# Attention: score and meta products over 128 rows with zeros in the unused half, and raw weight buffers split by stage

## The chip, the cores and the metric

The kernel runs on one core of one Trainium2 chip. The metric is the device time of one execution in microseconds (us); less is better. The core has five engines that run side by side: TensorE (PE, matrix products; PEld is its loading of weights), VectorE (DVE), ScalarE (ACT), GpSimd (POOL) and SyncE (SP), which issues most DMA transfers.

## The reference, cut to what matters

One decoder block over 1,024 positions and 16 meta tokens ahead of them (1,040 keys), width 1,024: a norm, a recurrent branch and an attention branch with gates, an output projection, and an MLP. The attention has 8 heads; a head has two components of 64 dimensions, and its result is the difference of two softmaxes, applied to 128-wide values:

```
s = jnp.einsum('bqhcd,bkhcd->bhcqk', q, k) * scale        # c: the two components
p = jax.nn.softmax(jnp.where(mask, s, min), axis=-1)
p_diff = p[:, :, 0] - lam * p[:, :, 1]
return jnp.einsum('bhqk,bkhe->bqhe', p_diff, v)
```

## The kernel before, in words

Every float32 operand of a product is split into a high part and a low part of a shorter format, and a product is made of three: high by low, low by high, high by high (`mm3`). The stages follow one another: norm and transposition of the inputs, recurrent branch, its gate and projection, attention, merge, output projection, MLP.

**Weights.** `load_split` loads 1,024 numbers a partition (512 KB) into a raw buffer `w_raw` (two in turn, `WRAW`), has POOL write the high part `w_hi` and DVE (POOL in the attention stage) the low part `w_lo`, each with two buffers. `col_tile` hands out a tile and calls `load_ahead` for the next one, so loading runs one tile ahead of use. The second half of the output projection and `row_tile` of the MLP take raw buffers from the same pair.

**Scores.** The keys of a component are stored with their 64 high rows and their 64 low rows stacked in 128 rows (`k2`), and the queries' high part twice (`q2`), so that one product over 128 rows gives two of the three terms. The third one, the queries' low part by the keys' high part, runs over the 64 rows that hold them: `ql` has the low parts of both components stacked, component 0 in rows 0 to 63 and component 1 in rows 64 to 127. `scores` goes through a block of 128 queries in steps: each step is one `ql` product and one `q2` product into one of three banks (`take_s`), and a DVE instruction that adds the mask and takes the maximum. Then come the exponentials on ACT and the difference of the softmaxes on DVE (`s`).

**Values.** `turn` transposes the differences of two blocks of queries, `weigh` multiplies them by the values. The 16 meta tokens are handled apart: their high and low parts are stacked in 64 rows, and `weigh_meta` adds one product over 64 rows (`mt` by `vmt`).

**Order.** Within the attention stage PE's order is the program's order. Steps of the next head's projections (keys, values, queries, of 260 or 504 columns at a time) are placed between the steps of a head by tables written out by hand (`MAIN_FIRST`, `MAIN`, `MAIN_LAST`, `TAIL`). When a key or query projection ends, `rope` copies it, moves halves by DMA, and multiplies and adds on DVE and POOL. The other engines' order is set by a scheduler.

Of the kernel before, what the change touches and what calls it, by code (L numbers as in the profile page):

```python
# [11 lines left out]
F32 = mybir.dt.float32  # L12
F32R = mybir.dt.float32r
# [5 lines left out]
P = 128  # L19
# [14 lines left out]
# chunks of all positions and of those after the meta tokens, none across the halves  # L34
# [4 lines left out]
WRAW = 2  # L39
MZ = 464  # L40
# attention: the inputs of the next head are worked out in STEPS steps between the steps of a head;
# so many of them come after each step: of all its blocks but the last two (of the first head, of the
# last one and of the others), and of the last two. START: ahead of the first head; SPARE: kept from
# the last head for the merge
# [8 lines left out]
# steps of the second gate's projection ahead of the last sums  # L53
# [4 lines left out]
def _rope_tables():  # L58
    """cos and sin by (row of a head's two 64-wide components, position); the sine carries the
    sign of the rotation."""  # L60
    inv = (1.0 / (10000.0 ** (np.arange(0, HD, 2) / HD)).astype(np.float32)).astype(np.float32)
    ang = inv[:, None] * np.arange(T, dtype=np.float32)[None, :]
    c, s = np.cos(ang), np.sin(ang)
    return (np.concatenate([c, c, c, c]).astype(np.float32),
            np.concatenate([-s, s, -s, s]).astype(np.float32))
# [3 lines left out]
def hybrid_block(ctx: ExitStack, tc: tile.TileContext, x, meta_tokens, g_mix, w_in, conv_w, conv_b,  # L69
# [11 lines left out]
    def f32(ap):  # L81
        return ap.bitcast(F32)

    def banks_of(first, n):
        """takes the n banks of PSUM from the first on in turn; between two turns, the bank of the
        later one."""
# [19 lines left out]
    # columns of weights in the order of their use, loaded one tile ahead  # L106
# [44 lines left out]
    def mm3(o, pairs, first=True, last=True):  # L151
        """o += sum of lhsT.T @ rhs over pairs of split operands; the product of the two low parts
        lies below float32's last place."""
# [25 lines left out]
    def rstd_of(ssum, n, rows=P):  # L179
        """1 / sqrt(ssum / n + eps) of one number a partition."""  # L180
# [5 lines left out]
    # scratch in DRAM  # L186
# [6 lines left out]
    # of the heads' blocks of queries: sums of the exponentials  # L193
# [5 lines left out]
    with tc.tile_pool(name="hn", bufs=1) as hnp:  # L199
# [6 lines left out]
        with tc.tile_pool(name="pre", bufs=2) as pre:  # L206
            blocks = [(NM, 0, meta_tokens)] + [(P, NM + P * i, x[0, P * i:P * (i + 1), :]) for i in range(NB)]
            xts = []
            for i, (rows, col, src) in enumerate(blocks):
# [6 lines left out]
                if i == 4:  # L216
                    # per-channel vectors: rows of 128, turned into columns
# [40 lines left out]
            # 4 softplus(-lambda): log1p(e) = 2 atanh(e / (2 + e)) as a series in z <= 1/3  # L258
# [16 lines left out]
        def project_by(c0, chunks, take, use):  # L275
            """columns c0.. of w_in against positions, a step at a time; use(first, width, psum) takes
            each chunk."""
# [15 lines left out]
        with tc.tile_pool(name="yr", bufs=1, reuse_waits="tile") as yrp:  # L293
            yr = []
            with tc.tile_pool(name="rg", bufs=1, reuse_waits="tile") as rg, \
# [9 lines left out]
                for n in range(KT):  # L305
# [14 lines left out]
                    # gelu(x) = x sigmoid(2 sqrt(2/pi) (x + 0.044715 x^3))  # L320
# [19 lines left out]
                    # t = tanh(-log_a / 2): a = (1 - t) / (1 + t), sqrt(1 - a^2) = 2 sqrt(t) / (1 + t)  # L340
# [41 lines left out]
        with tc.tile_pool(name="atc", bufs=1, reuse_waits="tile") as atc, \  # L382
# [5 lines left out]
            # zeros, then a block of 128 with the keys after the row's own position masked  # L388
# [4 lines left out]
            # the differential weight  # L393
# [7 lines left out]
            # minus lambda, in column 0  # L401
# [6 lines left out]

            def rope(h, c0, chunks, done, E=G):
                """columns c0.. of w_in against positions, rotated by position."""  # L410
# [24 lines left out]
            def head_inputs(h):  # L435
                """keys, values and queries of a head, a step at a time."""
                # keys of a component: the 64 rows' high parts and low parts, stacked
                yield from rope(h, 3 * D + P * h, ALL, lambda t1: set_keys(h, t1))
                # values by position: high parts and low parts
# [12 lines left out]
                for step, _ in enumerate(rope(h, 2 * D + P * h, REAL, lambda t1: rot.update({h: t1}), V)):  # L452
# [5 lines left out]
                    for i, j in enumerate(js):  # L458
                        if j < NB:
                            transpose(o[:, i, :], vt[:, NM + P * j:NM + P * (j + 1)])  # L460
                        else:
                            transpose(o[:4 * NM, i, :], f32(vm).rearrange("p a b c -> p (a b c)"))
                            vt_meta[h] = at.tile([4 * NM, P], F32R, name="vmt", bufs=2)
                            A.copy(out=vt_meta[h], in_=o[:4 * NM, i, :])
# [5 lines left out]
            def queries(h):  # L470
                """queries of a component: the high parts twice; the low parts of both, stacked."""
                t1 = rot[h]
                q2 = [at.tile([P, S], F32R, name=f"q2{c}") for c in range(2)]
                ql = at.tile([P, S], F32R, name="ql")
                ques[h] = q2, ql
                for c, (own, oth) in enumerate(halfs):
                    A.copy(out=q2[c][own], in_=t1[own])
                    V.tensor_copy(out=q2[c][oth], in_=t1[own])
                    V.tensor_tensor(out=ql[own], in0=t1[own], in1=f32(q2[c][own]), op=ALU.subtract)

            def scores(h, b, st):
                """a block of queries against the keys, and the difference of its softmaxes."""
# [6 lines left out]
                for c in range(2):  # L489
                    s = at.tile([P, T], F32, name=f"s{c}", bufs=3 - c)  # L490
                    sc.append(s)
                    for i in range(np_):
# [3 lines left out]
                        q2, ql = ques[h]  # L496
                        own = halfs[c][0]
                        matmul(o[:, :wa], lhsT=ql[own, P * b:P * (b + 1)], rhs=keys[h][c][own, k0:k0 + wa],
                               start=True, stop=False)
                        matmul(o[:, :wa], lhsT=q2[c][:, P * b:P * (b + 1)], rhs=keys[h][c][:, k0:k0 + wa],  # L500
# [12 lines left out]
                # e0 - lambda (sum0 / sum1) e1: the difference times sum0  # L513
# [8 lines left out]
                # of the meta tokens: high parts twice, low parts twice  # L522
# [6 lines left out]
            def turn(p, g, st):  # L529
                """two blocks of keys of the differences of two blocks of queries, transposed; the  # L530
# [331 lines left out]
```

## Time and profile before

| | us |
|---|---|
| median of 3 runs (lowest to highest) | 2036.28 (2035.9 to 2040.91) |
| span of the profiled execution, first to last instruction | 2034.7 |
| time of the median run that is not in this span | 1.6 |
| PE busy in the span | 1964.6 (97%) |
| DVE busy | 1132.7 (56%) |
| ACT busy | 584.6 (29%) |
| POOL busy | 515.8 (25%) |

A busy PE is not a PE at its peak: matmuls are pipelined, and the record of one overlaps that of the next. Busy time tells where PE has work; how fast it works is read from the starts of its instructions. Idle time of another engine costs nothing as long as PE does not wait for it.

### The profile page before, as it was taken

To read this page: it belongs to the slowest core of one execution; us is meant where nothing else is said; L and a number is where in the kernel's file an instruction comes from. 1 tells how busy PE (TensorE), PEld (TensorE's weight loads), DVE (VectorE), ACT (ScalarE), POOL (GpSimd) and SP (SyncE) were. 2 spreads that over 40 slices of the span, in tenths; PEclk is the share of its full clock that TensorE was granted. 3 is DMA by queue.
4 is the path that set the end of the run, shared out by engine and by line. 5 is a ranking of instruction groups with operands and counts; after the bars stand their busy time and mean duration, and the time that the engine had idled before them with its cause. 6 is when DMAs were issued, how large, how long until landed. Compare 5 with 4: busy or idle time off the path is not lost.

```text
span 2034.7 us, 26093 instructions
## 1 busy us (share of the span) xinstructions
PE 1964.6 (97%) x10562; PEld 1651.9 (81%) x10562; DVE 1132.7 (56%) x1909; ACT 584.6 (29%) x1190; POOL 515.8 (25%) x364
## 2 busy tenths in 40 slices
PE   7989889999999999999999999999999999999998
PEld 6988888888778778878779888878888888888886
DVE  7788882113677677667752543444444444444446
ACT  5534440002444554445433220320011110001113
POOL 3355540016242333234203332010011100111102
PEclk9999999999899999999999999999999999999999
DMA  5111112132012111111206535021111111111202
GB/s 161 38 42 32 43 32 73 63 114 77 21 48 58 40 40 50 40 37 50 60 29 217 194 121 186 1 83 42 42 52 56 48 52 42 42 42 53 63 21 83
DMA packets 138154, 131.60 MB, mean 65 GB/s; under 512 B 6081, under 2 KB 118945, under 8 KB 138033
## 3 DMA queue, kind: packets, MB, share of 16 engines
q1 hardware_dynamic: 135664, 127.83, 20.2%
q10 hardware_dynamic: 2368, 2.10, 0.4%
q8 instruction: 83, 1.36, 0.3%
q14 instruction: 39, 0.31, 0.1%
HBM read 104.61 MB, written 16.84 MB: 60 GB/s over the span
## 4 chain that ended last, share of the span: by engine, by line
PE 79%; DVE 12%; issue 4%; ACT 2%; DMA 1%; POOL 1%; SPq 0%; DVEq 0%; ACTq 0%; POOLq 0%
PE bank L142 77%; PE bank L147 2%; DVE gate L345 2%; DVE t L422 1%; DVE s L519 1%; DVE xc L313 1%; DVE cf L517 1%; DVE xcl L318 1%; DVE s L503 1%; POOL gate L344 1%; DVE yr L368 1%; DVE fin L830 0%; DVE w_lo L103 0%; ACT L343 0%; ACT s L343 0%
## 5 line engine op out<-in xcount | busy, mean ns | idle before, releaser
L142 PE MATMUL bank<-act1l,w_hi 128*128 128x260 f32 (+1 forms) x1152 | 360.5, 313 | 3.8 <-ACT sg L359 2.9
L142 PE MATMUL bank<-act1h,w_lo 128*128 128x260 f32 (+1 forms) x1152 | 358.5, 311 | 0.0
L142 PE MATMUL bank<-act1h,w_hi 128*128 128x260 f32 (+1 forms) x1152 | 358.2, 311 | 0.0
L102 POOL TENSOR_SCALAR w_hi<-w_raw 128x1024 fp32r<-128x1024 f32 x108 | 135.0, 1250 | 805.7 <-PE bank L142 722.1
L142 PE MATMUL bank<-act0l,w_hi 128*128 128x260 f32 (+2 forms) x896 | 316.2, 353 | 0.0
L142 PE MATMUL bank<-act0h,w_lo 128*128 128x260 f32 (+2 forms) x896 | 311.5, 348 | 1.2 <-DVE w_lo L103 1.2
L142 PE MATMUL bank<-act0h,w_hi 128*128 128x260 f32 (+2 forms) x896 | 311.7, 348 | 0.0
L817 DVE TENSOR_TENSOR h<-bank,h 128x512 f32<-128x512 f32 x256 | 176.4, 690 | 200.1 <-PE bank L142 200.1
L142 PEld LDWEIGHTS bank<-act1l,w_hi 128*128 128x128 f32 x1152 | 221.8, 193 | 17.0 <-ACT sg L359 3.1
L142 PEld LDWEIGHTS bank<-act1h,w_lo 128*128 128x128 f32 x1152 | 221.4, 192 | 12.6
L142 PEld LDWEIGHTS bank<-act1h,w_hi 128*128 128x128 f32 x1152 | 221.3, 192 | 11.7
L795 ACT ACTIVATE relu<-bank 128x512 f32<-128x512 f32 x64 | 38.3, 600 | 575.0 <-PE bank L142 555.2
L103 DVE TENSOR_TENSOR w_lo<-w_raw,w_hi 128x1024 fp32r<-128x1024 f32 x76 | 109.6, 1442 | 165.3 <-POOL w_hi L102 165.3
L142 PE MATMUL bank<-w_l,ff_h 128*128 128x512 f32 x512 | 200.5, 392 | 0.0
L142 PE MATMUL bank<-w_h,ff_h 128*128 128x512 f32 x512 | 200.5, 392 | 0.0
L142 PE MATMUL bank<-w_h,ff_l 128*128 128x512 f32 x512 | 199.4, 390 | 0.0
L142 PEld LDWEIGHTS bank<-act0h,w_hi 128*128 128x128 f32 x896 | 170.3, 190 | 21.6
L142 PEld LDWEIGHTS bank<-act0h,w_lo 128*128 128x128 f32 x896 | 170.6, 190 | 20.6 <-ACT sq L234 1.4
L142 PEld LDWEIGHTS bank<-act0l,w_hi 128*128 128x128 f32 x896 | 170.4, 190 | 18.8 <-DVE act0l L252 0.3
L784 POOL TENSOR_SCALAR w_h<-w_raw 128x1024 fp32r<-128x1024 f32 x32 | 34.0, 1065 | 516.3 <-PE bank L142 295.6
L503 DVE CUSTOM_DVE_ANT_0 s<-bank,mask 128x144 f32<-128x144 f32 (+6 forms) x224 | 113.0, 507 | 91.4 <-PE bank L142 90.3
L511 ACT ACTIVATE s<-s,m 128x272 f32<-128x272 f32 (+7 forms) x128 | 100.0, 784 | 63.2 <-DVE m L509 58.1
(243 smaller groups left out, 3355.3 us busy)
## 6 DMA issues: line engine op xcount, KB each, us to landing
w_raw<-in_w_ff SPq DMA_DIRECT2D x64, 512.0 KB
w_raw<-in_w_in SPq DMA_DIRECT2D x56, 512.0 KB
sw<-raw SPq DMA_DIRECT2D x32, 130.0 KB
xt<-in_x SPq DMA_DIRECT2D x8, 512.0 KB
w_raw<-in_w_rnn_out SPq DMA_DIRECT2D x8, 512.0 KB
mr_d<-sg SPq DMA_DIRECT2D x8, 512.0 KB
sw<-raw SPq DMA_DIRECT2D x32, 128.0 KB
u_d<-u SPq DMA_DIRECT2D x32, 128.0 KB
```

The lines of the kernel that those rows point to most:

```text
L102: G.tensor_scalar(out=hi, in0=raw, scalar1=1.0, scalar2=0.0, op0=ALU.mult, op1=ALU.add)
L103: low_part[0].tensor_tensor(out=lo, in0=raw, in1=f32(hi), op=ALU.subtract)
L142: i = PE.matmul(*args, **kw)
L147: i = PE.transpose(o, x, ident[:x.shape[0], :x.shape[0]])
L313: V.scalar_tensor_tensor(out=xc, in0=xp[:, k:k + T], scalar=par[:, 8 * k + n:8 * k + n + 1], in1=xc, op0=ALU.mult, op1=ALU.add)
L318: V.tensor_tensor(out=xcl, in0=xc, in1=f32(xch), op=ALU.subtract)
L345: V.reciprocal(out=rt, in_=rt)
L503: V.tensor_tensor_reduce(out=s[:, k0:k0 + w], in0=o[:, :w], in1=mask[:, m0:m0 + w], op0=ALU.add, op1=ALU.max, scale=1.0, scalar=MASK, accu ...
L511: A.activation(out=sc[c][:, :L], in_=sc[c][:, :L], func=AF.Exp, scale=0.125, bias=m2[:, c:c + 1], accum_out=sums[c][:, h, b:b + 1])
L784: G.tensor_scalar(out=hi, in0=raw, scalar1=1.0, scalar2=0.0, op0=ALU.mult, op1=ALU.add)
L795: A.activation(out=r, in_=o, func=AF.Relu)
L817: V.tensor_tensor(out=h2[t][:, es], in0=o, in1=h2[t][:, es], op=ALU.add)
```

## The change

The low parts of the queries get a tile per component (`qls`), of 128 rows, whose unused half is set to zero once ahead of the heads; the product then runs over all 128 rows of the keys, the stacked low rows being multiplied by zeros. The meta tokens' tiles (`vmts`, two in turn, and `mt`) get 128 rows too, the last 64 of them zero. These tiles live for the whole stage. The raw buffer of `load_split` becomes a single one (`WRAW = 1`), the output projection gets two raw buffers of its own and the MLP's `row_tile` one. Comments are removed throughout; the tables of the order stay.

```diff
-WRAW = 2
+WRAW = 1
...
+            qls = [atc.tile([P, S], F32R, name=f"ql{c}") for c in range(2)]
+            vmts = [atc.tile([P, P], F32R, name=f"vmt{i}") for i in range(2)]
+            mt = atc.tile([P, 2 * P], F32R, name="mt")
+            for t, rows in [(qls[c], halfs[c][1]) for c in range(2)] + [(t, halfs[0][1]) for t in (*vmts, mt)]:
+                G.memset(f32(t[rows]), 0.0)
...
-                            vt_meta[h] = at.tile([4 * NM, P], F32R, name="vmt", bufs=2)
-                            A.copy(out=vt_meta[h], in_=o[:4 * NM, i, :])
+                            vt_meta[h] = vmts[h % 2]
+                            A.copy(out=vt_meta[h][:4 * NM], in_=o[:4 * NM, i, :])
...
-                ql = at.tile([P, S], F32R, name="ql")
-                ques[h] = q2, ql
+                ques[h] = q2
                 for c, (own, oth) in enumerate(halfs):
                     A.copy(out=q2[c][own], in_=t1[own])
                     V.tensor_copy(out=q2[c][oth], in_=t1[own])
-                    V.tensor_tensor(out=ql[own], in0=t1[own], in1=f32(q2[c][own]), op=ALU.subtract)
+                    V.tensor_tensor(out=qls[c][own], in0=t1[own], in1=f32(q2[c][own]), op=ALU.subtract)
...
-                        q2, ql = ques[h]
-                        own = halfs[c][0]
-                        matmul(o[:, :wa], lhsT=ql[own, P * b:P * (b + 1)], rhs=keys[h][c][own, k0:k0 + wa],
+                        matmul(o[:, :wa], lhsT=qls[c][:, P * b:P * (b + 1)], rhs=keys[h][c][:, k0:k0 + wa],
                                start=True, stop=False)
-                        matmul(o[:, :wa], lhsT=q2[c][:, P * b:P * (b + 1)], rhs=keys[h][c][:, k0:k0 + wa],
+                        matmul(o[:, :wa], lhsT=ques[h][c][:, P * b:P * (b + 1)], rhs=keys[h][c][:, k0:k0 + wa],
                                start=False, stop=True)
...
-                st["mt", p] = at.tile([4 * NM, 2 * P], F32R, name="mt", bufs=1)
-                A.copy(out=st["mt", p], in_=o)
+                A.copy(out=mt[:4 * NM], in_=o)
...
-                matmul(st["acc"], lhsT=vt_meta[h], rhs=st["mt", p], start=False, stop=True)
+                matmul(st["acc"], lhsT=vt_meta[h], rhs=mt, start=False, stop=True)
...
-                    raw = wp.tile([P, 1024], F32, name="w_raw", bufs=WRAW)
+                    raw = wo.tile([P, 1024], F32, name="wo_raw", bufs=2)
...
-                    raw = wp.tile([P, 1024], F32, name="w_raw", bufs=WRAW)
+                    raw = ml.tile([P, 1024], F32, name="w2_raw", bufs=1)
```

## Rows read from the trace of the kernel before

**Rows 1.** Busy time of each engine in stretches of the span: a middle head, the MLP, and two stretches of 8 us in the first and in the last head. The columns are start and end, length, then busy time and number of instructions of PE, PEld, DVE, ACT and POOL, the clock granted to TensorE as a share of full speed, the DMA's share and GB/s.

```profile
667.80:739.50 71.70, 69.84 (x447) 57.78 (x447) 52.03 (x138) 34.24 (x82) 24.36 (x19) 1.00 0.17 45
1327.00:2010.00 683.00, 682.90 (x2961) 556.15 (x2962) 309.35 (x438) 81.31 (x137) 76.91 (x63) 1.00 0.16 47
...
500.00:508.00 8.00, 6.60 (x39) 5.08 (x39) 7.01 (x16) 2.26 (x10) 7.63 (x3) 1.00 0.46 118
1042.00:1050.00 8.00, 6.61 (x38) 5.13 (x38) 6.93 (x13) 2.91 (x6) 3.32 (x4) 1.00 0.38 131
```

**Rows 2.** Groups of PE's instructions in the attention stage (busy us and mean ns of one, then the idle time before them), and the two kinds of 64-row products with count, shortest, median and longest duration in ns, first and last start.

```profile
L142 PE MATMUL bank<-k,q 128*128 128x456 f32 x32 | 15.2, 475 | 0.0
L142 PE MATMUL bank<-k,ql 64*128 64x456 f32 x32 | 15.1, 471 | 0.0
...
L142 PE MATMUL bank<-k,ql x224: 369/420/639, 498.5 to 1056.8; 64*128 64x264 f32 x16, 64*128 64x328 f32 x16, 64*128 64x392 f32 x16, 64*128 64x456 f32 x16
L142 PE MATMUL bank<-mt,vmt x32: 379/382/579, 520.4 to 1075.5; 64*128 64x256 f32 x32
```

**Rows 3.** PE's instructions in order of time around score products of 456 columns: start, duration (us), engine, line, operands, shapes. The `act` rows are steps of a projection with 504 columns.

```profile
609.44 0.39 PE L142 MATMUL bank<-act0h,w_hi 128*128 128x504 f32 x1
609.76 0.47 PE L142 MATMUL bank<-k,ql 64*128 64x456 f32 x1
610.16 0.47 PE L142 MATMUL bank<-k,q 128*128 128x456 f32 x1
610.57 0.47 PE L142 MATMUL bank<-k,ql 64*128 64x456 f32 x1
...
611.77 0.47 PE L142 MATMUL bank<-k,q 128*128 128x456 f32 x1
612.08 0.39 PE L142 MATMUL bank<-act0l,w_hi 128*128 128x504 f32 x1
612.31 0.39 PE L142 MATMUL bank<-act0h,w_lo 128*128 128x504 f32 x1
```

**Rows 4.** The same view around a product of the meta tokens, all of 256 columns.

```profile
606.74 0.28 PE L142 MATMUL bank<-ptl,v 128*128 128x256 f32 x1
606.95 0.38 PE L142 MATMUL bank<-mt,vmt 64*128 64x256 f32 x1
607.26 0.28 PE L142 MATMUL bank<-sqh,ones 128*1 128x256 f32 x1
607.38 0.28 PE L142 MATMUL bank<-sql,ones 128*1 128x256 f32 x1
```

**Rows 5.** Weight loading, in order of time on several engines (in brackets the engine's idle time before the instruction and what ended it): high and low part of a tile and the next high part in the stage after the recurrent branch; a transfer in the MLP (SPq is its issue) and the work that waited for it; the memset of the mask. The last row is one of the chain of work that ended last, with the time of the first transfers.

```profile
339.31 1.05 POOL L102 TENSOR_SCALAR w_hi<-w_raw 128x1024 fp32r<-128x1024 f32 x1 [10.10 <-PE bank L142]
340.39 1.23 DVE L103 TENSOR_TENSOR w_lo<-w_raw,w_hi 128x1024 fp32r<-128x1024 f32 x1 [0.37 <-POOL w_hi L102]
350.55 1.05 POOL L102 TENSOR_SCALAR w_hi<-w_raw 128x1024 fp32r<-128x1024 f32 x1 [10.19 <-PE bank L142]
...
1341.58 0.34 SPq L783 DMA_DIRECT2D w_raw<-in_w_ff  x1
1345.36 1.05 POOL L784 TENSOR_SCALAR w_h<-w_raw 128x1024 fp32r<-128x1024 f32 x1 [5.07 <-DMA w_raw<-in_w_ff]
...
441.00 0.60 POOL L390 MEMSET mask<- 128x592 f32 x1
...
2.12 6.24 DMA xt<-in_x
```

**Rows 6.** A middle head around the end of the next head's key projection. First the busy times of two stretches, columns as in rows 1, then the score products of the queries' low parts alone in the first of them (PE, PEld, DVE); then instructions in order of time.

```profile
726.00:738.20 12.20, 11.02 (x67) 8.75 (x66) 12.13 (x25) 5.05 (x15) 8.55 (x6) 1.00 0.38 99
738.20:756.00 17.80, 17.80 (x105) 13.80 (x104) 11.55 (x39) 9.43 (x20) 8.55 (x6) 1.00 0.11 33
...
726.00:738.20 12.20, 2.81 (x7) 1.28 (x7) 0.00 (x0) 1.00 0.38 99
...
726.17 1.05 POOL L102 TENSOR_SCALAR w_hi<-w_raw 128x1024 fp32r<-128x1024 f32 x1 [15.53 <-PE bank L142]
727.49 3.30 DVE L422 TENSOR_TENSOR t<-raw,cos 128x1040 f32<-128x1040 f32 x1
733.45 2.87 DVE L519 SCALAR_TENSOR_TENSOR s<-s,cf,s 128x400 f32<-128x400 f32 x1
737.43 0.76 DVE L519 SCALAR_TENSOR_TENSOR s<-s,cf,s 128x528 f32<-128x528 f32 x1
737.56 0.41 PE L142 MATMUL bank<-k,ql 64*128 64x328 f32 x1 [1.18 <-DVE mx L503]
738.16 0.63 PE L147 MATMUL bank<-ident,s 128*128 128x128 f32 x4
```

**Rows 7.** Two waits of PE and the granted clock behind them (the column ahead of the last two of the busy times): in the first head, then in the recurrent stage.

```profile
509.49 0.55 PE L147 MATMUL bank<-ident,s 128*128 128x128 f32 x3 [2.89 <-DVE s L519]
510.00:512.00 2.00, 2.00 (x14) 1.97 (x13) 1.23 (x7) 1.07 (x3) 0.00 (x0) 0.66 0.00 0
512.00:521.00 9.00, 9.00 (x31) 6.67 (x28) 3.76 (x15) 4.31 (x10) 5.08 (x4) 0.51 0.00 0
...
120.84 0.43 PE L142 MATMUL bank<-xcl,gw0h 128*128 128x348 f32 x1 [2.64 <-DVE xcl L318]
120.00:128.00 8.00, 7.16 (x43) 7.16 (x44) 6.48 (x5) 2.95 (x6) 0.00 (x0) 0.79 0.22 65
```

## Prediction

> **What bounds the kernel now.** I read the busy time by stage first [rows 1]: TensorE (PE) is busy for 69.84 of the 71.70 us of a middle head and for 682.90 of the 683.00 us of the MLP, so the attention stage moves almost one for one with PE. The edit's matmuls lie only there, between 498 and 1076 us [rows 2]. VectorE (DVE) is next, 52.03 of 71.70 us in a head; ScalarE and GpSimd (POOL) are half idle. The reader is to see that 19.7 us per head is all that DVE leaves free.
>
> Next, what PE's time consists of. By the groups of PE's work [rows 2], a product over 64 rows lasts as long as one over 128: 471 against 475 ns for 456 columns. A duration is not yet a price, since matmuls overlap, so the third view is PE's order in time, start to start [rows 3]. Between full products of 504 columns a start follows the last after 0.23 us (0.454 ns a column; 456 columns would be 0.207). Around a 64-row product the steps are longer: projection to `ql` 0.32 (0.09 too long), `ql` to `q` 0.40 (0.19 too long), `q` to the next `ql` 0.41 (0.20), `q` to a projection 0.31 (0.10). In the same rows no later full product shows an excess. The meta tokens' product [rows 4] shows the same twice: 0.21 and 0.31 us where a 256-column step takes 0.12, so 0.09 + 0.19 = 0.28. What these steps have in common is a change of the number of rows, before and after each such product. I take the excess for the price of that change.
>
> **What the change removes.** Every `ql` product is followed by a full `q` product in the kernel's own order, so each of the 224 [rows 2] changes the rows twice. A pair alone costs 0.09 + 0.19 + 0.10 = 0.38 us too much, a pair in a row of pairs 0.19 + 0.20 = 0.39: I take 0.40, as all steps are rounded to 0.01. That is 224 x 0.40 = 89.6 us, and 32 x 0.28 = 9.0 us for the meta tokens: 98.6 us of PE time, 12.3 in each of the eight heads (28 x 0.40 + 4 x 0.28). The lower bound for one pair is nothing (if the steps have another cause), the upper one 0.42 (each of its three steps 0.01 longer).
>
> A rule of the Trainium skill speaks against the change. Its page TensorE: Matmul & The Clock Gate, in the section Part 3: Packing small matmuls, says that products over few rows that lie on different row groups of the array run side by side; padding gives that up. By that rule the two components' low products, if they are paired today, are half hidden. The rows show the contrary order: the components' low products are never neighbours, and the step from `ql` to `q` is twice the columns' time [rows 3]. So the sum goes by the rows.
>
> **What it adds.** Rows of zeros cost no column: nothing, between 0 and 4 ns a product (475 minus 471), so at most 0.9 us in all. The subtraction into `qls` and the copies into `mt` and `vmts` keep shapes and count. Five memsets run once on POOL, ahead of the first head; the one of 592 columns took 0.60 us [rows 5], so two of 1,024 columns are about 1.0 each (an estimate from that row) and three small ones 0.2 to 0.3 each: 2.8 us, in a stretch where POOL sits waiting 10.10 us for PE [rows 5]. Without that cover it would be 2.8 us, once.
>
> The single raw buffer of `load_split` is the edit that could bite. Before, the transfer of tile k+2 starts when the low part of k is done; now it is that of k+1. Behind that transfer in SyncE's queue stand the rope's copies and the stores, but all those issued later belong to work that follows tile k on PE, which needs k's low part as well; so they are not held. In the stage with the shortest tiles the high part starts at 339.31, the low part at 340.39 and ends at 341.62; the next high part runs at 350.55, released by PE [rows 5]. A transfer took 3.78 us from its issue at 1341.58 to the work that waited for it at 1345.36; the slowest that I saw on the chain was 6.24 [rows 5]. So the tile lands between 345.4 and 347.9, at least 2.6 us ahead of need. I price it at nothing; without cover it would cost its lateness on each of some 100 tiles. The separate buffers of the output projection and of the MLP replace shares of the old pair; PE never waits for either there, so nothing, with the same slack.
>
> **Where PE's gain is not kept.** In each middle head there is a stretch, 726.0 to 738.2 us, in which DVE is busy for 12.13 of 12.20 us [rows 6]. It begins when the next head's key projection ends: that frees POOL's weight split and the rope's multiplication on DVE, which takes 3.30 us beside POOL's work, as does one softmax difference with 2.87 us. At its end PE waits 1.18 us for a score bank, and the transposition at 738.16 starts as the difference needed for it ends (737.43 + 0.76 = 738.19). PE's work in the stretch holds 7 pairs [rows 6] and one meta product: 7 x 0.40 + 0.28 = 3.1 us. Shortening it only lengthens the wait, from 1.18 to about 4.3 us. What is late next is the next head's keys and so nothing on PE. The rest of the head, 12.3 - 3.1 = 9.2 us, I take as kept: DVE has pauses there (after the stretch it is busy for 11.55 of 17.80 us). Both ends for this term: all 3.1 kept, or DVE holding PE in other places too.
>
> Six middle heads give 6 x 9.2 = 55.2 us. In the first and the last head PE already waits for DVE in several places (busy for 6.60 of 8.00 us from 500, for 6.61 of 8.00 from 1042 [rows 1]), so I take half of the 12.3 for each: 12.3 together. Sum: 67.5 us.
>
> **The clock.** A longer wait can cost more than itself. After a wait of 2.89 us at 509.49 the granted clock was 0.66, then 0.51 of full until 521, that is the lower of its two levels, 1.2 GHz [rows 7]: 0.34 x 2 + 0.49 x 9 = 5.1 us of work lost. After a wait of 2.64 us at 120.84, in the recurrent stage, it was 0.79 over 8 us: 1.7 us lost. Waits of 1.18 us left it at 1.00. So seven waits of 4.3 us (one in every head that has a next one) will probably each lower it. I take 1.7, since the work behind the waits is dense there as in the recurrent stage: 7 x 1.7 = 11.9 us, with 0 and 5.1 as ends. Expected gain: 67.5 - 11.9 = 55.6 us.
>
> **Rivals.**
> 1. Nothing is lost: the order on DVE gives way, and all 98.6 us come through: 1937.7 us. For it: PE alone is nearly full in [rows 1]. Against: the stretch in [rows 6].
> 2. The waits take more: the clock stays low for 5.1 us after each of the seven waits, or waits for DVE's differences open elsewhere too. Gain 67.5 - 35.7 = 31.8 us: 2004.5 us. For it: the wait at 509.49; against: the milder fall at 120.84.
> 3. The steps have another cause, such as the banks: no change, 2036 us. Against: the meta product shows the same steps on another bank [rows 4].
> 4. Slower: the single raw buffer. It decides once a transfer takes over 8.9 us (350.55 - 341.62); to eat up 55.6 us over some 100 tiles it has to take 9.5, and at 11 us the lateness of 2.1 us a tile makes 210 - 55.6 = 154 us more, 2191 us. Against it: 3.78 and 6.24.
> 5. Slower: the low products do overlap their neighbours today. If the 112 second ones were hidden, padding would add 112 x 0.207 = 23 us: 2059 us. It would need steps shorter than 0.207 beside a `ql`; rows 3 have 0.32 and 0.40. This is what the Trainium skill's rule on packing, named above, would make of it.
>
> **How the numbers follow.** The profiled span is 2034.7 us, 1.6 below the median of the runs, 2036.3 (2035.9 to 2040.9); the same 1.6 lies around it after. 2036.3 - 55.6 = 1980.7 us. Chances: the forecast, with the clock's fall between none and 3 us a wait (1968 to 1990), 0.52; rival 1 and what lies near it 0.15; rival 2 0.27; rival 3 0.03; rival 4 0.02; rival 5 0.01. The range goes from 1942, near rival 1, to 2010, past rival 2. About 0.3% (6 us) is what runs of this kernel can tell from no change; faster than that 0.94, same 0.03, slower 0.03.
>
> **What the profile after would show.** Right: the steps around `ql`, now 128 rows, of about 0.21 us for 456 columns, and 0.12 for the meta product; a middle head of 62 to 64 us, not 71.7; in it one wait of 3 to 5 us before the fourth score product of a block, after a stretch of full DVE; a granted clock below 1.00 behind it; the stages outside 498 to 1076 us as long as now. Wrong: steps of 0.40 that stay (rival 3); a head of 59 us with no longer wait (rival 1); PE waiting for weights, POOL for `w_raw` in the stages with short tiles (rival 4). The forecast fails most easily in the two terms that the rows can't fix: how DVE's order shifts against PE, and how long the clock stays low.

## The result, and the profile after

The changed kernel takes 1978.6 us (median of 4 runs, 1977.1 to 1981.7) where the kernel before took 2036.1 beside it: 0.9716 of its time, 95% interval 0.9700 to 0.9732, faster by 57.5 us. The profiled execution has a span of 1979.9 us, 54.8 less than before.

All of it comes from the attention stage. Busy times of stretches, columns as in [rows 1]. First the kernel before, from the last product of the stage ahead to the last product of the meta tokens:

```profile
450.50:1075.50 625.00, 605.22 (x3796) 501.31 (x3794) 416.83 (x1102) 276.96 (x662) 211.38 (x161) 0.98 0.17 48
```

Then the kernel after: the same stage, a middle head, and the stretch in which DVE is full, which answers to [rows 6].

```profile
449.00:1018.40 569.40, 523.00 (x3795) 497.27 (x3794) 421.67 (x1102) 276.57 (x662) 215.79 (x166) 0.96 0.19 53
785.74:851.19 65.45, 60.99 (x446) 58.50 (x446) 51.86 (x139) 34.22 (x82) 24.42 (x19) 0.94 0.18 50
838.20:848.50 10.30, 6.59 (x52) 6.26 (x52) 10.23 (x20) 4.43 (x14) 7.29 (x5) 0.91 0.45 117
```

The stage is 55.6 us shorter; the MLP takes 682.70 us, as long as it did [rows 1]. PE's busy time falls by 82.2 us; what it stands idle grows from 19.8 to 46.4 us, by 26.6, and 82.2 - 26.6 is the 55.6. The busy time holds a second loss. Summed over windows of 10 us, each counted as 10 us times what the granted clock lacks to 1.00, the clock's falls take 10.2 us in the stage before and 20.4 after. At one clock the products therefore became shorter by 82.2 + 10.2 = 92.4 us; 26.6 of that went into waits and 10.2 into the clock. These are the two profiled executions. That of the kernel after has the lowest mean clock of its four runs (0.982; the others 0.984 and 0.985). Taken as the span times what the mean granted clock lacks to 1.00, the four lose 31.6 us on average and 23 runs of the kernel before 26.1, so over all runs the clock takes some 5 or 6 us more than before, by this estimate, not 10.

That the products changed as meant is seen in the order of time, after. Score products of 456 columns, then a meta product, with the columns of [rows 3, 4]; last the group of the low products with count, shortest, median and longest duration.

```profile
863.59 0.37 PE L142 MATMUL bank<-k,q 128*128 128x456 f32 x1
863.79 0.37 PE L142 MATMUL bank<-k,ql 128*128 128x456 f32 x1
864.00 0.36 PE L142 MATMUL bank<-k,q 128*128 128x456 f32 x1
...
841.24 0.28 PE L142 MATMUL bank<-mt,vmt 128*128 128x256 f32 x1
841.35 0.28 PE L142 MATMUL bank<-sqh,ones 128*1 128x256 f32 x1
...
L142 PE MATMUL bank<-k,ql x224: 275/338/642, 497.0 to 1000.5; 128*128 128x264 f32 x16, 128*128 128x328 f32 x16, 128*128 128x392 f32 x16, 128*128 128x456 f32 x16
```

The steps are 0.20 and 0.21 us, where [rows 3] had 0.40 and 0.41, and 0.11 behind the meta product, where [rows 4] had 0.31. What else a change of the number of rows does is seen in the loading of weights. First two loads of the kernel before, around the products of [rows 3], then one of the kernel after:

```profile
609.76 0.18 PEld L142 LDWEIGHTS bank<-k,ql 64*128 64x128 f32 x1 [0.36 <-issue]
610.16 0.19 PEld L142 LDWEIGHTS bank<-k,q 128*128 128x128 f32 x1 [0.22 <-issue]
...
863.59 0.19 PEld L142 LDWEIGHTS bank<-k,ql 128*128 128x128 f32 x1
```

Before, these weights begin to load only when their own product begins (609.76 and 610.16 in [rows 3]), after 0.36 and 0.22 us in which nothing is loaded. After, the weights of the `ql` product of 863.79 load from 863.59 on, under the product ahead of it. So a part of the excess is a load that nothing covers; how large a part, no run separates.

Where the gain is given back stands in the stretch of full DVE. After, in order of time; then the granted clock (third column from the right) in a stretch of 2 us.

```profile
837.98 2.41 POOL L103 TENSOR_TENSOR w_lo<-w_raw,w_hi 128x1024 fp32r<-128x1024 f32 x1
838.17 3.31 DVE L428 TENSOR_TENSOR t<-raw,cos 128x1040 f32<-128x1040 f32 x1
841.56 2.43 POOL L429 TENSOR_TENSOR sw<-sw,sin 128x1040 f32<-128x1040 f32 x1 [1.17 <-DVE t L428]
842.30 1.70 DVE L520 SCALAR_TENSOR_TENSOR cf<-sum,lam,cf 128x1 f32<-128x1 f32 x1
844.04 2.84 DVE L522 SCALAR_TENSOR_TENSOR s<-s,cf,s 128x400 f32<-128x400 f32 x1
848.13 0.64 PE L142 MATMUL bank<-k,ql 128*128 128x328 f32 x1 [3.71 <-DVE mx L506]
...
848.00:850.00 2.00, 1.87 (x8) 1.83 (x9) 2.00 (x10) 0.12 (x2) 0.00 (x0) 0.50 0.00 0
```

The wait at the fourth score product of block 4 is 3.71 us, where [rows 6] had 1.18; the clock is at 0.50, its lower level of 1.2 GHz, from 846.6 to 853.6.

### The profile page after: what moved, and what is told of

Same layout as the page of the kernel before. It is cut to its first block, busy times and chain, and to the rows that moved or that the text cites. A ratio compares the mean times of both kernels' runs of the same rounds, so it can differ in the third digit from the quotient of the medians.

```text
span 1979.9 us, 26085 instructions
## 1 busy us (share of the span) xinstructions
PE 1882.0 (95%) x10562; PEld 1647.4 (83%) x10562; DVE 1139.2 (58%) x1909; ACT 584.5 (30%) x1190; POOL 517.3 (26%) x369
## 4 chain that ended last, share of the span: by engine, by line
PE 73%; DVE 16%; issue 5%; ACT 3%; POOL 1%; DMA 1%; SPq 0%; POOLq 0%; DVEq 0%; ACTq 0%
PE bank L142 71%; DVE gate L345 2%; PE bank L147 2%; DVE s L506 2%; DVE s L522 2%; DVE cf L520 2%; DVE t L428 1%; DVE xc L313 1%; ACT s L514 1%; DVE xcl L318 1%; DMA sw<-raw 1%; DVE ql L484 1%; POOL gate L344 1%; POOL sw L429 0%; DVE m L512 0%
## 5 line engine op out<-in xcount | busy, mean ns | idle before, releaser
L142 PEld LDWEIGHTS bank<-act0h,w_lo 128*128 128x128 f32 x896 | 172.2, 192 | 20.4 <-ACT sq L234 1.4
```

What stands on the lines that cost most here:

```text
L142: i = PE.matmul(*args, **kw)
```

## The experiments

Ratios are to the kernel before, run beside each of them.

**1. The raw buffer alone.**

```
-WRAW = 2
+WRAW = 1
...
-                    raw = wp.tile([P, 1024], F32, name="w_raw", bufs=WRAW)
+                    raw = wo.tile([P, 1024], F32, name="wo_raw", bufs=2)
...
-                    raw = wp.tile([P, 1024], F32, name="w_raw", bufs=WRAW)
+                    raw = ml.tile([P, 1024], F32, name="w2_raw", bufs=1)
```

> The kernel before with the third edit alone: one raw buffer of weights, and two rings of their own for the later weights. The prediction priced it at nothing: 2036.1 us, within 2. A rival from the trace of after, where the gate projection behind the last head waits 2.0 us once for POOL's w_lo: plus 1.5, and at most plus 6 if the wait comes back in other stages. The rival with the serial loads, 2191.

Measured: 2038.1 us beside 2037.9, ratio 1.0007 (0.9995 to 1.0019). No difference that these runs can tell. The one wait foreseen is there, though. PE's waits in this kernel behind the last head (total, times, longest), then the place in the kernel after:

```profile
PE bank L142 <- POOL w_lo L103: 2.0, 1, 2.0
```

```profile
1058.03 0.39 SPq L101 DMA_DIRECT2D w_raw<-in_w_attn_out  x1
1068.85 1.60 POOL L102 TENSOR_SCALAR w_hi<-w_raw 128x1024 fp32r<-128x1024 f32 x1 [11.81 <-DMA w_raw<-in_w_attn_out]
1073.25 0.50 PE L142 MATMUL bank<-ya0h,w_lo 128*128 128x512 f32 x1 [2.01 <-POOL w_lo L103]
```

There a transfer takes 10.8 us from its issue to the work that waits for it, and the loads of the merge go on beside it. The edit brings one wait of 2.0 us that the kernel before doesn't have; the runs, with 0.2 us between the medians, can tell it neither from nothing nor from 2.

**2 and 3. Each kind of product alone.** In the first, from the kernel after, the meta tokens' products go back to 64 rows; in the second, the queries' low products.

```
-                matmul(st["acc"], lhsT=vt_meta[h], rhs=mt, start=False, stop=True)
+                matmul(st["acc"], lhsT=vt_meta[h][:4 * NM], rhs=mt[:4 * NM], start=False, stop=True)
```

```
-                        matmul(o[:, :wa], lhsT=qls[c][:, P * b:P * (b + 1)], rhs=keys[h][c][:, k0:k0 + wa],
+                        own = halfs[c][0]
+                        matmul(o[:, :wa], lhsT=qls[c][own, P * b:P * (b + 1)], rhs=keys[h][c][own, k0:k0 + wa],
```

> The changed kernel with the meta tokens' products back on 64 rows. The theory that each switch of the row form costs its own 0.28 us: 32 x 0.28 = 9.0 us of TensorE come back, less what waits swallow: 1984 to 1988 us. The rival that these lone products cost nothing where a wait stands near: 1978.6, within 2.

> The changed kernel with the low products of the queries back on 64 rows; only the meta tokens' products are padded. The theory of additive excess: 2036.1 less 9.0 = 2027 us, 2026 to 2030. If the 32 products cost nothing on the path: 2036.

Measured: the queries' products alone 1981.9 us, 0.9735 (0.9717 to 0.9754); the meta tokens' alone 2033.9 us, 0.9987 (0.9973 to 1.0001). Nearly all the gain is the queries'. Both times fall between the two forecasts made for them, so all four missed. Giving the meta products up costs 3.3 us by the medians, not 9.0, and the two intervals overlap (0.9717 to 0.9754, 0.9700 to 0.9732). The meta products alone bring 2.7 us by the ratio, not 9.0, and the interval just includes no gain. Why, the attention stage with the meta products alone shows, and below it one stretch of 20 us in it:

```profile
448.60:1072.50 623.90, 602.38 (x3796) 507.00 (x3795) 418.46 (x1102) 277.58 (x662) 214.45 (x166) 0.97 0.17 48
...
650.00:670.00 20.00, 18.67 (x109) 15.47 (x109) 16.72 (x42) 7.83 (x21) 8.57 (x6) 0.91 0.23 59
```

and the same stretch of the kernel before:

```profile
650.00:670.00 20.00, 18.91 (x122) 15.47 (x121) 17.10 (x45) 8.49 (x22) 8.85 (x7) 1.00 0.23 59
```

The products did get shorter: PE's busy time in the stage falls by 2.8 us and the clock's falls, 17.1 us against 10.2, hide 6.9 more, 9.7 in all for the 9.0 priced. But 1.7 of it turned into idle time and 6.9 into clock. Four of the six middle heads, all at 1.00 in the kernel before, now fall once (8.6 us together), the first head loses 3.4 us more, and a fall of 5.1 us in the last head is gone. How much of this the edit does is not shown, as one execution stands against one. In the profile of experiment 1, whose attention stage is that of the kernel before, the falls take 13.7 us, a middle head's among them; and by the mean clocks of all the runs the kernel with the meta products alone loses 29.1 us and the kernel before 26.1, which is 3 us and not 6.9.

**4. The low product twice.** From the kernel before: every low product of the queries is run twice in a row on the same 64 rows.

```
+                        matmul(o[:, :wa], lhsT=ql[own, P * b:P * (b + 1)], rhs=keys[h][c][own, k0:k0 + wa],
+                               start=False, stop=False)
```

> The kernel before with each low product of the queries run twice in a row on the same 64 rows, so the low parts count twice in the scores. A head's low products have 9,696 columns, 77,568 in the eight heads, which at 0.42 to 0.45 ns a column are 32 to 35 us. If the excess is the switch into and out of the 64-row form, the second one steps by about 0.45 ns a column (0.21 us at 456 columns) and the kernel takes 2060 to 2071 us. If the excess belongs to each product of 64 rows (0.40 us), 224 x 0.40 = 90 us more come on top: 2140 to 2160.

Measured: 2072.4 us beside 2037.9, so 34.5 us more (ratio 1.0182, 1.0161 to 1.0203): 0.445 ns a column, as any full product. The difference lies in the 32 to 35 us forecast; the time is 1 us above its range, since the kernel before ran 1.8 us slower beside it. A second 64-row product behind a first has no excess; the excess is the change of the form.

**5. A neighbour on the other rows.** From the kernel before: ahead of the low product, one on the other 64 rows, into a bank that nobody reads, in blocks 0, 1, 2 and 4.

```
+                        oth = halfs[c][1]
+                        if b in (0, 1, 2, 4):
+                            matmul(take_a()[:, :wa], lhsT=ql[oth, P * b:P * (b + 1)], rhs=keys[h][c][oth, k0:k0 + wa],
+                                   start=True, stop=True)
```

> The kernel before with one more product of 64 rows ahead of the low product in ten chunks a head (blocks 0, 1, 2 and 4): it uses the other 64 rows, goes to a bank that nobody reads, and is left out of the result. If neighbouring products on different rows overlap, the low product behind it begins 0.02 to 0.05 us later; if they follow each other as any two, at 0.42 to 0.45 ns a column (0.12 us for 264 columns, 0.15 for 328). The whole: 80 products of 23,936 columns in all, 10.7 us by the second way, a few us by the first.

Products of 328 columns in order of time: a lone low product (before), two on the same rows (experiment 4), two on different rows (this one).

```profile
664.01 0.41 PE L142 MATMUL bank<-k,ql 64*128 64x328 f32 x1
664.35 0.42 PE L142 MATMUL bank<-k,q 128*128 128x328 f32 x1
```

```profile
667.40 0.56 PE L142 MATMUL bank<-k,ql 64*128 64x328 f32 x2
667.89 0.42 PE L142 MATMUL bank<-k,q 128*128 128x328 f32 x1
```

```profile
676.18 0.41 PE L142 MATMUL bank<-k,ql 64*128 64x328 f32 x2
676.52 0.42 PE L142 MATMUL bank<-k,q 128*128 128x328 f32 x1
```

From the first low product to the full one: 0.34, 0.49 and 0.34 us. Two products on different halves of the rows take the time of one. The rule on packing that the prediction weighed (the Trainium skill, TensorE: Matmul & The Clock Gate, Part 3: Packing small matmuls) holds in this trace. The kernel before just had no such neighbours. Packing two chunks' low products would still pay the form's change: by these rows three products' time and 0.38 us against four products' time, which at 0.445 ns a column pays only above 850 columns a chunk (an estimate), and no chunk here has more than 456. The time, 2073.0 us, is 36 us above the kernel before, where at most 10.7 were forecast. It is that of a single run and says little: the added products wait for their bank, 17.8 us in all, and the clock falls more often.

**6. The keys' cosines to POOL.** From the kernel after.

```
-                        V.tensor_tensor(out=t1[:, ts], in0=raw[:, ts], in1=cos[:, ts], op=ALU.mult)
+                        E.tensor_tensor(out=t1[:, ts], in0=raw[:, ts], in1=cos[:, ts], op=ALU.mult)
```

> The changed kernel with the keys' product with the cosines on POOL, not on DVE. If DVE's full stretch sets the wait of 3.7 us at the fourth score product of block 4, the stretch is shorter by that product's 3.3 us, the wait falls below 1 us and the clock stays up: 7 heads x (3 + 2) = 35 us at best, 1945 to 1965 us. If POOL's longer work slows the DVE operations beside it by as much, or another wait takes the place: 1978, within 4.

Measured: 2001.9 us, 0.9824 (0.9803 to 0.9844), 23 us slower than the kernel after; both expectations missed. The wait grew to 5.67 us. POOL and DVE in order of time, and the wait:

```profile
786.31 2.41 POOL L103 TENSOR_TENSOR w_lo<-w_raw,w_hi 128x1024 fp32r<-128x1024 f32 x1
786.48 2.25 DVE L520 SCALAR_TENSOR_TENSOR cf<-sum,lam,cf 128x1 f32<-128x1 f32 x1
788.68 2.42 POOL L429 TENSOR_TENSOR sw<-sw,sin 128x1040 f32<-128x1040 f32 x1
788.77 2.76 DVE L522 SCALAR_TENSOR_TENSOR s<-s,cf,s 128x400 f32<-128x400 f32 x1
791.20 2.56 POOL L430 TENSOR_TENSOR t<-t,sw 128x1040 f32<-128x1040 f32 x1
791.57 2.37 DVE L528 CAST dm<-s 128x32 fp32r<-128x32 f32 x1
796.21 0.64 PE L142 MATMUL bank<-k,ql 128*128 128x328 f32 x1 [5.67 <-DVE mx L506]
```

Each of these three DVE operations, even that on one number a row, ends with POOL's or up to 0.4 us behind it: 788.73 and 788.72, 791.53 and 791.10, 793.94 and 793.76. It doesn't run slower; it stands until POOL is done. This doesn't hold for every operation: in the kernel after, those that take the maximum of a score bank need 0.42 us beside POOL's product with the sines, as they do elsewhere. So DVE's full stretch is partly a stretch of standing still, and handing POOL more work lengthens it. The Trainium skill says as much (SBUF — State Buffer, section SBUF: two separate sides): the port pair that the two engines share is "an exclusive lock, not a bandwidth split". The trace agrees.

**7. Projection steps moved into the wait.** From the kernel after, the middle heads' table only.

```
-MAIN = (0, 1, 0, 11, 1, 0, 0, 0, 1, 1, 0, 8, 0, 2, 1, 2, 0, 0, 1, 5, 1, 0, 0, 1, 2, 8, 0, 0, 2, 0, 0, 1, 0,
-        3, 0, 0, 0, 0, 2, 0, 1, 0, 1, 5, 5, 4)
+MAIN = (0, 1, 0, 11, 1, 0, 0, 0, 1, 1, 0, 8, 0, 2, 3, 5, 5, 0, 1, 5, 1, 0, 0, 1, 2, 2, 0, 0, 2, 0, 0, 1, 0,
+        3, 0, 0, 0, 0, 2, 0, 1, 0, 1, 1, 5, 4)
```

> The changed kernel with ten projection steps of each middle head moved ahead of the products that wait, in front of the last three score products of block 4; they come from behind blocks 5 and 7. Ten steps take about 3.5 us of TensorE. If the idle time there is the loss, six heads win up to 3.5 us each and the 2 us of the clock: 1945 to 1958 us. If the wait goes to where the steps were taken from: 1976 to 1980.

Measured: 2003.9 us, 0.9832 (0.9812 to 0.9853), 25 us slower than the kernel after; both expectations missed. PE's waits in the attention stage, this kernel, then the kernel after:

```profile
PE bank L141 <- DVE ptl L546: 26.3, 18, 2.9
PE bank L141 <- DVE vm L453: 16.0, 6, 2.8
PE bank L146 <- DVE s L521: 14.1, 11, 4.3
PE bank L141 <- DVE mx L505: 5.3, 8, 2.2
```

```profile
PE bank L142 <- DVE mx L506: 28.2, 13, 3.8
PE bank L142 <- DVE ptl L547: 8.5, 8, 2.9
PE bank L147 <- DVE s L522: 8.4, 5, 4.0
```

The wait for score banks falls from 28.2 to 5.3 us as meant, and three others grow by 39.5. The steps fill banks that DVE must empty too (`vm` is new), and DVE is what lacks time there.

**8 and 9. Work without use in the wait.** Two trials from the kernel after. In the first the products go to the bank of the weighed sums, in all heads; in the second to a bank of the turned blocks, in the middle heads:

```
+                        if b == 4 and c == 1 and i == 1 and 0 < h < NH - 1:
+                            idle = take_t()
+                            for n in range(16):
+                                matmul(idle, lhsT=ques[h][0][:, :P], rhs=ques[h][0][:, :512], start=True, stop=True)
```

> The changed kernel with 16 full-row products of 512 columns (3.4 us by 0.42 ns a column), written to a bank that nobody reads, ahead of the waiting product in each head. They are no part of the result and do no useful work: the wait stays as long as it was, and only TensorE's activity in it changes. If the clock's falls come from this wait, they go, and what they took comes back: about 2.0 us a head in seven heads, 1963 to 1968 us. If the falls have another cause: 1978, or up to 1985 where the products outlast the wait.

> The changed kernel with 16 full-row products of 512 columns (3.5 us) ahead of the waiting product in the six middle heads, written to a bank that the turning of blocks uses and whose last reader is long done, so that they needn't wait themselves. Nobody reads what they write; the wait of 3.7 us becomes work without use. If TensorE's idle time there is what takes its clock down, the falls of the six heads vanish (2.4 us each by the windows of after) and 1962 to 1970 us come out. If the falls stay, 1978 to 1983.

Measured: 2005.4 us, 0.9843 (0.9818 to 0.9869), and 2009.0 us, 0.9859 (0.9841 to 0.9877). Both missed, and neither separates the clock from the wait as it should. In the first, 12.9 us of waits for the bank's reader came in. By the mean clocks its four runs lose 26.6 us, where the kernel after loses 31.6: some 5 us came back, where 14 were forecast. The second loses 33.1, no less than the kernel after. In it the wait was filled, and the next product that needs DVE, 8 us behind it, waited as long:

```profile
724.80 0.42 PE L142 MATMUL bank<-k,ql 128*128 128x328 f32 x1 [0.41 <-DVE mx L510]
732.43 0.58 PE L142 MATMUL bank<-ptl,v 128*128 128x256 f32 x1 [3.66 <-DVE ptl L551]
```

In the 10 us from 734 on the clock is 0.77. The fall moved with the wait; that it follows the wait is so far supported, that idle time alone causes it is not shown. What the runs do show: in the middle heads PE's added time is paid in full and more, some 30 us for 6 x 16 products (21 us at 0.22 each), although 6 x 3.7 = 22 us of waits stood there to be filled.

**10 to 12. POOL's operations to DVE.** From the kernel after. The keys' rotation on DVE:

```
-                        G.tensor_tensor(out=sw[:, ts], in0=sw[:, ts], in1=sin[:, ts], op=ALU.mult)
-                        E.tensor_tensor(out=t1[:, ts], in0=t1[:, ts], in1=sw[:, ts], op=ALU.add)
+                        (V if E is G else G).tensor_tensor(out=sw[:, ts], in0=sw[:, ts], in1=sin[:, ts], op=ALU.mult)
+                        V.tensor_tensor(out=t1[:, ts], in0=t1[:, ts], in1=sw[:, ts], op=ALU.add)
```

Run 10 adds the low parts of the weights, issued on DVE six projection steps late. Run 11 adds the low parts of the keys as well, and the queries' product with the sines. Run 12 has the keys' rotation and the keys' low parts alone:

```
-                G.tensor_tensor(out=k2[c][oth], in0=t1[own], in1=f32(k2[c][own]), op=ALU.subtract)
+                late.append([4 + 2 * c, lambda c=c, own=own, oth=oth: V.tensor_tensor(
+                        out=k2[c][oth], in0=t1[own], in1=f32(k2[c][own]), op=ALU.subtract)])
...
                     if k == KT - 1:
                         use(t0, n, o)
+                    for e in late:
+                        e[0] -= 1
+                    while late and late[0][0] <= 0:
+                        late.pop(0)[1]()
                     yield
```

> The changed kernel with the POOL operations of the full stretch on DVE: the keys' product with the sines, the keys' sum, and the low parts of the attention's weights, each of these issued on DVE six projection steps after its load. In the trace of after each of the three takes 2.4 us on POOL, and a DVE operation on tiles in the chip's memory beside it ends only when POOL's does (the cosines' product 3.31 us, 842.30's 128x1 operation 1.70, the softmax difference behind it 2.84), while the same sum takes 1.22 us on DVE alone. If POOL's operations hold DVE up, the stretch of 10.3 us shrinks to 7 or 8 us, the wait of 3.7 us falls below 1.5, and with the clock's falls 3 to 4 us a head come back in seven heads: 1948 to 1960 us. If DVE is full by its own work, its 6 to 7 us more a head (five operations at 1.2) find other waits: 1978 to 1990.

> The changed kernel with every two-input operation of the attention's inputs on DVE, none on POOL: the rotations of keys and queries, the low parts of the weights and of the keys (these two issued some projection steps after what they read). In the run with part of them moved, the wait of 3.7 us at block 4 fell to 0.65, and a new one of 3.84 stood behind the low parts of the keys on POOL (5.36 us, beside which a DVE operation of 64 numbers a row took 2.38). If those two POOL operations are the cause, the new wait goes as well: two waits and two falls of the clock a head against the run with part of them moved, 1999 less 7 x 5 = 1964, 1950 to 1972 us. If DVE's own work is now too much (eight operations at 1.2 us, some 10 us a head, in place of POOL's), 1995 to 2020.

> As the run before, but only the keys' rotation and the keys' low parts are on DVE; the low parts of the weights and the queries' product with the sines stay on POOL (2.4 us each). By the theory that POOL's two-input operations hold DVE up, it lies between that run and the changed kernel: the weights' low parts still collide with the keys' product with the cosines (3.31 us in the trace of after): 1965 to 1978 us. If DVE's own work decides, 1985 to 2000.

Measured: run 10 1999.3 us, 0.9809 (0.9789 to 0.9829); run 11 1986.7 us, 0.9748 (0.9722 to 0.9775); run 12 1965.6 us, 0.9644 (0.9620 to 0.9667). Runs 10 and 11 missed both of their forecasts; run 12 came in at the lower end of its first one. Run 12 is faster than the kernel after, whose interval (0.9700 to 0.9732) it doesn't touch, by some 13 us. Run 10, in order of time:

```profile
656.74 0.42 PE L147 MATMUL bank<-k,ql 128*128 128x328 f32 x1 [0.65 <-DVE mx L513]
658.10 5.36 POOL L446 TENSOR_TENSOR k<-t,k 64x1040 fp32r<-64x1040 f32 x2 [8.51 <-ACT k L445]
658.14 2.38 DVE L536 TENSOR_TENSOR dm<-s,dm 128x32 fp32r<-128x32 f32 x1
661.26 0.90 PE L152 MATMUL bank<-ident,s 128*128 128x128 f32 x3 [3.84 <-DVE s L529]
```

The wait for the score bank falls from 3.71 to 0.65 us although DVE has more work of its own, so POOL's hold was its cause. But the keys are ready earlier, their low parts now collide instead, and 4.5 us further on PE waits 3.84. Run 11, without any of these on POOL:

```profile
716.68 1.24 DVE L446 TENSOR_TENSOR k<-t,k 64x1040 fp32r<-64x1040 f32 x1
717.95 0.77 DVE L530 SCALAR_TENSOR_TENSOR s<-s,cf,s 128x528 f32<-128x528 f32 x1
718.78 0.55 PE L150 MATMUL bank<-ident,s 128*128 128x128 f32 x3 [3.03 <-DVE s L530]
```

Nothing stands any more, and PE waits 3.03 us all the same: the softmax difference `s` now queues behind the other work on DVE. So the theory that POOL's hold alone decides falls; it missed this run's range by 15 us. Run 12, and its attention stage:

```profile
699.72 3.31 DVE L432 TENSOR_TENSOR t<-raw,cos 128x1040 f32<-128x1040 f32 x1
708.20 0.42 PE L142 MATMUL bank<-k,ql 128*128 128x328 f32 x1 [2.23 <-DVE mx L511]
...
448.70:1003.00 554.30, 517.65 (x3796) 491.31 (x3795) 423.89 (x1134) 276.09 (x662) 138.13 (x134) 0.98 0.19 54
```

Of the three long holds that the kernel after shows (3.31, 1.70 and 2.84 us) only that of the cosines is left: the wait is 2.23 us, and the clock falls less (11.9 us, not 20.4), and the stage is 15.1 us shorter than after. Which of the two operations that run 11 moved in addition costs its 21 us, the low parts of the weights or the queries' product with the sines, stays open.

## Why the prediction was right

It said 1980.7 us in 1942 to 2010, with DVE's full stretch and the clock taking nearly half of the gain; 1978.6 came. Its sum against the stage:

- *The products*, 98.6 us priced, 92.4 measured. The mechanism is shown: the excess belongs to the change between 64 and 128 rows (experiment 4). The pair was rounded up, from 0.38 or 0.39 to 0.40 (and its upper bound should read 0.41, three steps of 0.01 above 0.38); the queries' share comes out at (92.4 - 9.0) / 224 = 0.37. A rule of the Trainium skill (TensorEngine Tiling (Array Packing), Key Properties) says the same, that "Changing tiling mode (not just tile) drains the TensorE"; the trace agrees, and the figure is the trace's.
- *The added work* at nothing: right but for the raw buffer, whose wait of 2.0 us comes once (experiment 1). The bound of 6.24 us for a transfer was too low at one place, where it took 10.8.
- *The waits*, 6 x 3.1 + 12.3 = 30.9 us priced, 26.6 measured. The wait in the six middle heads is 3.63 to 3.81 us, where 4.3 was forecast, at the product named. The seventh of the waits, in the first head, is only 1.74 us there.
- *The clock*, 11.9 us priced for seven falls, 10.2 measured in the profiled execution. That is not the sum that was forecast: six falls in the middle heads take 15.4 us, and 5.1 us of an old fall in the last head are gone. Over all runs it is some 5 or 6 us.

That the total is within 2 us is partly luck: two misses offset each other. By the starts of the queries' low parts on DVE (569.08 to 999.91 before, 562.93 to 958.04 after) a middle head became 5.95 us shorter, where 9.2 - 1.7 = 7.5 was forecast. Three terms are behind this: 11.9 us removed, not 12.3; 3.3 us of idle time, not 3.1 (the six middle heads are idle 5.04 us on average after, 1.70 before); 2.6 us of clock, not 1.7. The first and the last head together gained 4.65 + 15.2 = 19.9 us, where 12.3 - 1.7 = 10.6 was forecast. The prediction gave up half of the 12.3 us in each of them, without a row that fixes the half. In the first head that was right: its idle time grows by 5.6 us. In the last one it grows by only 1.0, so nearly all of the shorter products was kept. And the last head had a fall of its own in the kernel before, behind a wait of only 0.74 us at 1013.63, with 0.50 granted from 1016 to 1026, of which one stretch:

```profile
1016.00:1018.00 2.00, 2.00 (x6) 1.27 (x5) 0.84 (x5) 1.33 (x4) 0.00 (x0) 0.50 0.00 0
```

After, the clock is 1.00 in the whole last head: 5 us that the prediction didn't count, as it looked for falls that come and not for falls that go. That the shorter products took this fall away is not shown. It is there in experiment 1, and gone in experiment 3, where the queries' products are the old ones and the wait is 0.72 us.

The rivals. Nothing lost (1937.7) falls with the wait of 3.71. The waits taking more (2004.5) was the nearer one, but the clock cost 2.6 us a middle head, not 5.1. Another cause falls with experiment 4, the raw buffer with 1. The overlap of low products exists (experiment 5), not between the products of this kernel. Of what the profile should show, all came but one: a middle head takes 65.85 us, not 62 to 64.

## What to carry to other kernels

Price a small matmul by the steps around it, not by its duration: here a change between 64 and 128 rows cost 0.37 us a pair, and rows of zeros nothing. A gain on the busiest engine is kept only as far as the next engine follows: take off what the stretches with both full will swallow, then what the clock takes behind the longer waits, and look for falls that are there already and may vanish. Where DVE is full, first see how much of it stands still beside POOL: moving the keys' rotation and low parts from POOL to it gave 13 us more, moving every two-input operation of the heads' inputs lost 8.

## What the hardware showed unexpectedly

- A DVE operation on one number a row took 2.25 us beside POOL's subtraction for the weights' low part, and 0.21 to 0.22 elsewhere: it stands until POOL ends. One that reads a score bank took 0.42 us beside POOL as elsewhere.
- Two products on different 64 rows take the time of one (0.34 us for 328 columns), two on the same rows 0.49.
- Where the number of rows changes from one product to the next, the weights load only as the product begins (609.76, 610.16); between products of 128 rows they load under the product ahead (863.59 for the one of 863.79).
- The clock's fall doesn't follow the length of a wait. Behind 0.74 us it was at 0.50 for 10 us (before), and behind 0.72 us at the same place it didn't fall (experiment 3). Around a wait of 2.86 us in the first head it was at 0.50 for 7 us after, and around one of 2.85 at the same place before it stayed at 1.00.
